# GLU weights placed elsewhere, convolution steps spread over the S5 out-projection, and the first final norm at low priority, in a hybrid convolution/S5 encoder block

## The chip, the cores and the metric

The kernel runs on one core of a Trainium2 chip. The metric is the device time of one execution in microseconds; several executions are timed and the median is given. One more execution is recorded by the hardware profiler, and all rows shown here come from that one.

## The reference

One block, batch 1, 2048 positions and 16 learned meta tokens ahead of them, model width 1024:

```
z = rms_norm(h) ;  p = z @ w_in          # columns: conv value | conv gate | S5 input, 512 each
u = v * sigmoid(gate)
y = depthwise_conv(u, width 31) + conv_b # 512 channels
conv_out = silu(layer_norm(y))           # statistics over all 512 channels of a position
s5 = gelu(S5(ssm_u) + d * ssm_u)         # bidirectional state space model
ssm_out = s5 * sigmoid(s5 @ glu_w + glu_b)
h = h + concat(conv_out, ssm_out) @ w_out
h = h + relu(rms_norm(h) @ w_ff1)^2 @ w_ff2
out = rms_norm(h)                        # meta positions dropped
```

All matrix products keep float32 accuracy: each operand is split into a high part (a cast to a shorter float, on ScalarE) and a low part (the difference, on VectorE), and three products are added (high·high, high·low, low·high).

## The kernel before

Engines are named as in the profile: PE is TensorE, DVE VectorE, ACT ScalarE, POOL GpSimd, SP the engine whose queue issues most transfers. Each engine, and each DMA queue, takes its instructions in the order in which they stand. That order is made by a scheduler: the program is written in one order, each piece gets a priority from its place there, and a piece with `tc.high_priority` is drawn forward.

The stages follow each other: input projection, S5 scan and the products for gate and value `v` (to about 495 us of the span); the stage called P3 here (495 to 820 us), which the change rewrites; then two halves of 1024 positions, each with the first FFN product (`hid_pair`), the second one (`second`) and the final norm (`final`). The first half ends at about 1505 us.

P3 works on four blocks of 512 positions (`blk` 0 to 3), and every block has four tiles of 128. Its parts are these:

- `load_glu` brings the GLU weights in by SP (`raw_gw`) and splits them into `gw` (helper `split`, lines 141 and 142).
- `conv_quad(q)`, q from 0 to 15, does the convolution of 32 channels for all positions as 12 matmuls against band matrices `cb`; four adds then write the result with its bias into the four tiles `cv`. A profile counts 24 PE records for one quad. `u8` is the input, read back from DRAM (`vdr`). `toeplitz(h)` clears a `cb` buffer and fills it with 8 transfers; one serves two quads.
- `s5_out(blk)` reads the S5 result `y`, applies the GELU (`ga`), splits it (`ghl`), multiplies by `gw` (192 matmuls `glu` over the four blocks), applies the gate (`gb`), splits again (`mhl`) and calls `wout_mm(0, ...)`.
- `wout_mm(top, blk, ...)` multiplies by one half of w_out (`woh`, `wol`, from `load_wout`; 96 matmuls `wo` for a block). Per tile it loads `xo` (the residual, 3 buffers shared with others), adds the product on DVE (line 45) and stores `xo`, to `pdr` in the S5 half (top 0) and to `hdr` in the convolution half (top 1).
- `ln_out(blk)` is the LayerNorm and swish. It needs the result of all 16 quads, since the statistics (`bn_stats`) run over all channels. It normalises `cv` (line 59), turns it by 16 transposes `tr_ln` on PE, makes `lzz` by two DVE operations (lines 59 and 45) and splits that into `zc`, the low part on POOL.
- `z_step` is the next norm with its transposes `trf` (line 836), inside the second half of w_out.

In the program before, all 16 quads are written ahead of the four `s5_out`. `gw` lies in the pool P3R, on the right side of SBUF, where the weights of the value products and their staging tiles `stv` lay. Four `cb` buffers take the tags `za` and `zb` (two each); the first half of w_out has tag `zb` too, so it waits until the quads have read `cb2` and `cb3`.

`final(half)` squares the eight accumulators `acc` on ACT, computes an inverse root on DVE, scales `acc` on DVE and stores it from SP. The FFN of the second half has its first weights (`sm`, `w`) prepared on DVE and ACT, the same engines.

Of the kernel before, what the change touches and what calls it, by code (L numbers as in the profile page):

```python
# [9 lines left out]
F32 = mybir.dt.float32  # L10
F32R = mybir.dt.float32r
# [7 lines left out]
P = 128  # L19
# [18 lines left out]
def hymba_kernel(ctx, tc, x, meta, norm_mix_g, w_in, conv_w, conv_b, conv_ln_g, conv_ln_b,  # L38
# [40 lines left out]
    def zslot(shape, name, dt=F32R, tag=None):  # L79

        if tag is None:
            tag = "zb" if nz[0] // 2 % 2 else "za"
            nz[0] += 1
        return PZ.tile(shape, dt, tag=tag, name=name, bufs=2)
# [30 lines left out]
    xv = x[0].rearrange("(c s) d -> s c d", s=NT)  # L115
# [46 lines left out]
    with ExitStack() as es2:  # L162
# [712 lines left out]
        with tc.tile_pool(name="p3", bufs=1, reuse_waits="tile") as P3:  # L875
# [3 lines left out]
            def t3(shape, name, bufs=1, dt=F32, tag=None, pool=None):  # L879
                return (pool or P3).tile(shape, dt, tag=tag or name, name=name, bufs=bufs)  # L880
# [3 lines left out]

            cv = [t3([P, 4, 512], f"cv{blk}", pool=(P3R if blk < 2 else P3)) for blk in range(4)]
            es3 = ExitStack()
            hlp = []

            def hl_tile(name):
                if not hlp:  # L890
                    hlp.append(es3.enter_context(tc.tile_pool(name="p3b", bufs=1, reuse_waits="tile")))
                return hlp[0].tile([P, 2, 512], F32R, tag="hl", name=name, bufs=9)

            def conv_quad(q):

                j = q // 4
                ps = ks_ps(f"cv{q}", [P, 4, 8, NT])
                u8 = t3([P, 4, W], f"u8_{q}", bufs=2, tag="u8", pool=P3R)
                SP.dma_start(u8, dap(vdr[j], (q % 4) * 32 * NT * W, [[W, P], [P * W, 4], [1, W]]))
                cb = toeplitz(q // 2) if q % 2 == 0 else cbs[q // 2 if q < 8 else q // 2 % 2]  # L900
                for i in range(4):
                    for m in range(3):
                        T.matmul(ps[:, i], u8[:, i, 2 - m:2 - m + P], cb[:, 4 * (q % 2) + i, :, ts(m, 16)],  # L903
                                 start=(m == 0), stop=(m == 2))
                bv = convb[:, 32 * q:32 * q + 32].rearrange("p (i c) -> p i c", c=8).unsqueeze(2)
                for blk in range(4):
                    o = cv[blk][:, :, 32 * q:32 * q + 32].rearrange("p t (i c) -> p i t c", c=8)
                    add(o, ps[:, :, :, 4 * blk:4 * blk + 4].rearrange("p i c t -> p i t c"),
                        bv.broadcast_to([P, 4, 4, 8]))
# [2 lines left out]

            def toeplitz(h):

                n = h if h < 4 else h % 2
                if h < 4:
                    cbs.append(zslot([P, 8, 8, 48], f"cb{h}", F32, tag="za" if h < 2 else "zb"))
                    (GP if h % 2 else V).memset(cbs[h], 0.0)
                for c in range(8):
                    SP.dma_start(cbs[n][16 * c:16 * c + 16, :, c, :],  # L920
                                 dap(edr[h // 2], (64 * (h % 2) + c) * 63, [[1, 16], [8 * 63, 8], [1, 48]]))
                return cbs[n]

            wo = {}

# [27 lines left out]
            def load_glu():  # L953
                for k in range(2):
                    r = raw4([P, 2, 512], f"raw_gw{k}")
                    SP.dma_start(r, glu_w[0][256 * k:256 * (k + 1), :].rearrange("(k p) n -> p k n", p=P))
                    w = t3([P, 2, 1024], f"gw{k}", dt=F32R, pool=P3R)
                    split(w[:, 0, :], w[:, 1, :], r.rearrange("p k n -> p (k n)"))
                    gw.append(w.rearrange("p a (k n) -> p a k n", k=2))

            def s5_out(blk):
                y, gh_ = [], []
                for j in range(4):
                    yy = t3([P, 512], f"y{blk}_{j}", tag="y", bufs=4)
                    SP.dma_start(yy, ydr[j][:, 4 * blk:4 * blk + 4, :].rearrange("p t c -> p (t c)"))
                    a = t3([P, 512], f"ga{blk}_{j}", tag="sg", bufs=2)
                    S.activation(a, yy, AF.Square)
                    tsc(a, a, 0.044715, ALU.mult, 1.0, ALU.add)
                    mul(a, a, yy)
                    S.activation(a, a, AF.Sigmoid, scale=1.5957691216057308)  # L970
                    mul(yy, yy, a)
                    g_ = hl_tile(f"ghl{blk}_{j}")
                    split(g_[:, 0, :], g_[:, 1, :], yy)
                    y.append(yy)
                    gh_.append(g_)
                mh = []
                for j in range(4):
                    ps = mm_ps(f"glu{blk}_{j}")
                    for k in range(4):
                        mm3(ps, gw[k // 2][:, 0, k % 2, ts(j, P)], gw[k // 2][:, 1, k % 2, ts(j, P)],  # L980
                            gh_[k][:, 0, :], gh_[k][:, 1, :], k == 0, k == 3)
                    a = t3([P, 512], f"gb{blk}_{j}", tag="sg", bufs=2)
                    S.activation(a, ps, AF.Sigmoid, bias=cols[:, 8 + j:9 + j])
                    mul(a, a, y[j])
                    m_ = hl_tile(f"mhl{blk}_{j}")
                    split(m_[:, 0, :], m_[:, 1, :], a)
                    mh.append(m_)
                wout_mm(0, blk, mh, xv, pdr)

            def ln_out(blk):  # L990
                mv = consts.tile([P, 4, 2], F32, name=f"mv{blk}", tag="mv", bufs=2)
# [22 lines left out]
                return zc  # L1014

            load_glu()
            for q in range(16):
                conv_quad(q)
                if q == 8:
                    load_wout(0)  # L1020
            load_wout(1)
            for blk in range(4):
                s5_out(blk)
            zcs = {0: ln_out(0)}
            for blk in range(4):
                if blk < 3:
                    zcs[blk + 1] = ln_out(blk + 1)
                if blk == 1:
                    esR.close()
                    PR = es5.enter_context(tc.tile_pool(name="pr", bufs=1, side="right", reuse_waits="tile"))  # L1030
                wout_mm(1, blk, zcs.pop(blk), pdr, hdr)
                if blk in (1, 2):
                    if blk == 1:
                        z_open(0)
                    for i in (0, 1) if blk == 1 else (2, 3):
                        z_step(0, i, lambda n: ks_ps(n, [P, 4, P]), lambda n: tr_ps(n, [P, 4, P]),
                               lambda q: t3([P, 512], f"zt0_{i}_{q}", tag="y", bufs=4))
# [135 lines left out]
    def final(half):  # L1173
        for t in range(8):
            n = f"{half}_{t}"
            ss, a, q, y, u, p = (consts.tile([P, 2 if i == 0 else 1], F32, tag=f"fin{i}", name=f"fin{i}_{n}", bufs=2)
                                 for i in range(6))
            h = acc[t]
            for nh in range(2):
                S.activation(junk[:, ts(nh, 512)], h[:, ts(nh, 512)], AF.Square, scale=1.0 / 32,  # L1180
                             accum_out=ss[:, nh:nh + 1])

            stt(a, ss[:, 0:1], EPS, ss[:, 1:2], ALU.add, ALU.add)
            tsc(q.bitcast(I32), a.bitcast(I32), 1, ALU.logical_shift_right)
            tsc(y.bitcast(I32), q.bitcast(I32), -1, ALU.mult, 0x5F3759DF, ALU.add)
            stt(q, y, a, y, ALU.mult, ALU.mult)
            stt(u, q, -3.0, y, ALU.add, ALU.mult)
            stt(q, u, a, u, ALU.mult, ALU.mult)
            tsc(p, q, -0.01171875, ALU.mult, 0.15625, ALU.add)
            tsc(p, p, q, ALU.mult, -0.9375, ALU.add)  # L1190
            mul(p, p, u)
            for nh in range(2):
                stt(h[:, ts(nh, 512)], h[:, ts(nh, 512)], p, gF[0][:, ts(nh, 512)], ALU.mult, ALU.mult)
                SP.dma_start(ov[8 * half + t][:, ts(nh, 512)], h[:, ts(nh, 512)])

    for half in range(2):
        with tc.tile_pool(name=f"p4_{half}", bufs=1, reuse_waits="tile") as P4:
            for p in range(NFF // 2):
                hid_pair(p, half, P4, "1267534" if p < NFF // 2 - 1 else "4312675",
                         z_late if p == 0 else None)  # L1200
        with tc.tile_pool(name=f"p5_{half}", bufs=1, reuse_waits="tile") as P5:
            second(half, P5, [(f, f + 1) for f in range(0, 8, 2)] + [(8,)] + [(f, f + 1) for f in range(9, 19, 2)] + [(19,)] +
                   [(f, f + 1) for f in range(20, 32, 2)] if half == 0 else [(f, f + 1) for f in range(0, 32, 2)])
            final(half)
    es5.close()


# [28 lines left out]
```

## Time and profile before

| what | value |
|---|---|
| three runs, us | 2186.47, 2184.84, 2182.39 (median 2184.84) |
| profiled execution, us | 2183.87, its span 2182.1 |
| PE busy | 2068.2 us (95% of the span), granted clock 0.980 on average |
| DVE busy | 1542.6 us (71%) |
| ACT, POOL busy | 710.6 us (33%), 160.5 us (7%) |

The span runs from the first to the last instruction; 1.8 us of the execution lie outside it. Busy shares are means over stages that differ: the page's slices show PE at nine tenths or more nearly everywhere, and lower ones at the beginning, around 500 to 600 us and near the final norms.

### The profile page before, as it was taken

What the parts mean: (1) busy time and instruction counts of PE and PEld (TensorE: products, weight loads), DVE (VectorE), ACT (ScalarE), POOL (GpSimd) and SP (SyncE); (2) the same over time, 40 slices, a digit from 0 to 9 for tenths busy, and PEclk for the clock granted to TensorE, in tenths of its full rate; (3) what the DMA queues carried; (4) which work ended last, traced back from release to release, by engine and by line L of the source; (5) the groups of instructions that cost most, each with busy time, mean ns of one, the idle gap of its engine ahead of it and who ended that gap; (6) DMA issues with size and microseconds to landing.
All of it is one profiled execution on the core that took longest, in us unless ns stands there. A gap on an engine that the chain in (4) does not pass through costs nothing.

```text
span 2182.1 us, 27333 instructions
## 1 busy us (share of the span) xinstructions
PE 2068.2 (95%) x10124; PEld 1694.4 (78%) x10124; DVE 1542.6 (71%) x2780; ACT 710.6 (33%) x1046; POOL 160.5 (7%) x242
## 2 busy tenths in 40 slices
PE   7989988898899999999999999997999999999997
PEld 5767777777777777888888888885888888888886
DVE  7866799963496487665558888869566656676767
ACT  5323222221143145444443222214444443111112
POOL 1031244500001110000000000000000000000000
PEclk9999999998899999999999999998999999999999
DMA  6245434423543666333345332524333235232322
GB/s 190 78 168 170 136 109 122 122 86 98 162 135 117 208 225 203 103 101 106 116 154 184 116 108 95 175 78 145 116 116 105 98 115 202 78 116 78 116 78 87
DMA packets 218509, 279.03 MB, mean 128 GB/s; under 512 B 31437, under 2 KB 164569, under 8 KB 217864
## 3 DMA queue, kind: packets, MB, share of 16 engines
q1 hardware_dynamic: 194024, 229.93, 34.2%
q10 hardware_dynamic: 23072, 43.10, 5.4%
q0 software_dynamic: 1280, 4.26, 0.5%
q8 instruction: 80, 1.31, 0.2%
q14 instruction: 53, 0.43, 0.1%
HBM read 195.39 MB, written 81.85 MB: 127 GB/s over the span
## 4 chain that ended last, share of the span: by engine, by line
PE 76%; DVE 12%; DMA 4%; issue 3%; ACT 1%; SPq 0%; ACTq 0%; POOL 0%; DVEq 0%; POOLq 0%
PE f L158 10%; PE f L159 10%; PE f L160 10%; PE ps L1093 10%; PE ps L1092 10%; PE ps L1091 9%; PE wo L158 2%; PE cv L903 2%; PE wo L160 2%; PE wo L159 2%; DMA h<-hdr 1%; DVE zo L756 1%; DVE zo L755 1%; DMA u<-udr 1%; DVE s L45 1%
## 5 line engine op out<-in xcount | busy, mean ns | idle before, releaser
L45 DVE TENSOR_TENSOR acc<-acc,f 128x512 f32<-128x512 f32 x496 | 331.7, 684 | 141.3 <-PE f L160 140.7
L158 PE MATMUL f<-w,hid 128*128 128x512 f32 x1024 | 399.9, 391 | 1.5 <-DVE acc L45 1.5
L159 PE MATMUL f<-w,hid 128*128 128x512 f32 x1024 | 398.9, 390 | 0.0
L160 PE MATMUL f<-w,hid 128*128 128x512 f32 x1024 | 398.7, 389 | 0.0
L1093 PE MATMUL ps<-zx,w 128*128 128x512 f32 x896 | 354.3, 395 | 11.7 <-DVE w L142 11.7
L1091 PE MATMUL ps<-zx,w 128*128 128x512 f32 x896 | 354.0, 395 | 5.6 <-ACT w L141 5.6
L1092 PE MATMUL ps<-zx,w 128*128 128x512 f32 x896 | 354.5, 396 | 0.0
L158 PEld LDWEIGHTS f<-w,hid 128*128 128x128 f32 x1024 | 192.3, 188 | 42.6 <-DVE acc L45 3.0
L160 PEld LDWEIGHTS f<-w,hid 128*128 128x128 f32 x1024 | 192.3, 188 | 40.1
L159 PEld LDWEIGHTS f<-w,hid 128*128 128x128 f32 x1024 | 192.3, 188 | 39.4
L1093 PEld LDWEIGHTS ps<-zx,w 128*128 128x128 f32 x896 | 169.5, 189 | 51.3 <-DVE w L142 12.7
L1091 PEld LDWEIGHTS ps<-zx,w 128*128 128x128 f32 x896 | 169.5, 189 | 45.6 <-ACT w L141 6.7
L1092 PEld LDWEIGHTS ps<-zx,w 128*128 128x128 f32 x896 | 169.4, 189 | 38.6
L141 ACT CAST hid<-rawh 128x1024 fp32r<-128x1024 f32 x64 | 67.3, 1052 | 360.9 <-PE f L160 351.5
L142 DVE TENSOR_TENSOR w<-sm,w 128x512 fp32r<-128x512 f32 x128 | 87.7, 690 | 65.9 <-ACT w L141 65.8
L141 ACT CAST w<-sm 128x512 fp32r<-128x512 f32 x128 | 78.7, 618 | 164.6 <-PE ps L1093 146.8
L141 ACT CAST w<-r 128x512 fp32r<-128x512 f32 x96 | 58.8, 616 | 130.6 <-PE ps L1093 130.5
L141 ACT CAST w<-raww 128x1024 fp32r<-128x1024 f32 x64 | 67.3, 1051 | 85.8 <-DMA raww<-in_w_ff_dram 85.8
L142 DVE TENSOR_TENSOR hid<-rawh,hid 128x1024 fp32r<-128x1024 f32 x64 | 78.2, 1222 | 15.7 <-ACT hid L141 15.7
L142 DVE TENSOR_TENSOR w<-raww,w 128x1024 fp32r<-128x1024 f32 x64 | 78.0, 1219 | 9.1 <-ACT w L141 9.1
L45 DVE TENSOR_TENSOR hh<-c,ps 128x512 f32<-128x512 f32 x64 | 44.0, 688 | 48.6 <-PE ps L1093 47.5
L45 DVE TENSOR_TENSOR xo<-xo,wo 128x512 f32<-128x512 f32 x64 | 43.8, 684 | 46.6 <-PE wo L160 43.3
(301 smaller groups left out, 3403.3 us busy)
## 6 DMA issues: line engine op xcount, KB each, us to landing
r<-in_w_ff_dram SPq DMA_DIRECT2D x64, 512.0 KB
fdr<-hh ACTq DMA_DIRECT2D x64, 512.0 KB
rawh<-fdr SPq DMA_DIRECT2D x64, 512.0 KB
raww<-in_w_ff_dram SPq DMA_DIRECT2D x64, 512.0 KB
h<-hdr SPq DMA_DIRECT2D x32, 512.0 KB
x<-in_x_dram SPq DMA_DIRECT2D x16, 512.0 KB
mt<-gdr SPq DMA_DIRECT2D x64, 128.0 KB
xo<-in_x_dram SPq DMA_DIRECT2D x16, 512.0 KB
```

The lines of the kernel that those rows point to most:

```text
L45: return V.tensor_tensor(out=o, in0=a, in1=b, op=op)
L141: S.copy(out=hi, in_=src)
L142: on.tensor_tensor(lo, src, hi.bitcast(F32), ALU.subtract)
L158: T.matmul(ps, lh, rh, start=first, stop=False)
L159: T.matmul(ps, lh, rl, start=False, stop=False)
L160: T.matmul(ps, ll, rh, start=False, stop=last)
L755: V.tensor_tensor_scan(zo[0:64, 2:4 * W + 2], f(rh)[0:64, :], f(zi)[0:64, :], 0.0, ALU.mult, ALU.add)
L756: V.tensor_tensor_scan(zo[64:128, 0:4 * W][:, ::-1], f(rh)[64:128, ::-1], f(zi)[64:128, ::-1], 0.0, ALU.mult, ALU.add)
L903: T.matmul(ps[:, i], u8[:, i, 2 - m:2 - m + P], cb[:, 4 * (q % 2) + i, :, ts(m, 16)], start=(m == 0), stop=(m == 2))
L1091: T.matmul(ps[q], w[q][:, 0, k], z[:, 0, k, :], start=(k == 0), stop=False)
L1092: T.matmul(ps[q], w[q][:, 0, k], z[:, 1, k, :], start=False, stop=False)
L1093: T.matmul(ps[q], w[q][:, 1, k], z[:, 0, k, :], start=False, stop=(k == 3))
```

## The change

The four edits are these. `gw` moves into a new pool P3G on the left side. The w_out half for the S5 part is loaded at the start and takes tag `zb`; only two `cb` buffers are left (tag `za`), and each is filled anew after the second quad that reads it. The quads are written four at a time behind the GLU of block 0 and behind the w_out products of blocks 0, 1 and 2. The final norm of the first half is wrapped in a priority with a negative offset, and its stores are issued by POOL (`GP`).

```diff
-            hlp = []
+            P3B = es3.enter_context(tc.tile_pool(name="p3b", bufs=1, reuse_waits="tile"))
+            esG = ExitStack()
+            P3G = esG.enter_context(tc.tile_pool(name="p3g", bufs=1, reuse_waits="tile"))
...
-                cb = toeplitz(q // 2) if q % 2 == 0 else cbs[q // 2 if q < 8 else q // 2 % 2]
+                cb = cbs[q // 2 % 2]
...
-                n = h if h < 4 else h % 2
-                if h < 4:
-                    cbs.append(zslot([P, 8, 8, 48], f"cb{h}", F32, tag="za" if h < 2 else "zb"))
-                    (GP if h % 2 else V).memset(cbs[h], 0.0)
+                n = h % 2
+                if h < 2:
+                    cbs.append(zslot([P, 8, 8, 48], f"cb{h}", F32, tag="za"))
+                    (GP if h else V).memset(cbs[h], 0.0)
...
+            def conv_four(n):
+                for q in range(4 * n, 4 * n + 4):
+                    conv_quad(q)
+                    if q % 2 and q < 12:
+                        toeplitz(q // 2 + 2)
...
-                    w = t3([P, 2, 1024], f"gw{k}", dt=F32R, pool=P3R)
+                    w = t3([P, 2, 1024], f"gw{k}", dt=F32R, pool=P3G)
...
-            def s5_out(blk):
+            def s5_glu(blk):
...
-                wout_mm(0, blk, mh, xv, pdr)
+                return mh
...
-            for q in range(16):
-                conv_quad(q)
-                if q == 8:
-                    load_wout(0)
-            load_wout(1)
+            load_wout(0)
+            for h in range(2):
+                toeplitz(h)
             for blk in range(4):
-                s5_out(blk)
+                mh = s5_glu(blk)
+                if blk == 0:
+                    conv_four(0)
+                if blk == 3:
+                    load_wout(1)
+                wout_mm(0, blk, mh, xv, pdr)
+                if blk < 3:
+                    conv_four(blk + 1)
...
-                SP.dma_start(ov[8 * half + t][:, ts(nh, 512)], h[:, ts(nh, 512)])
+                (SP if half else GP).dma_start(ov[8 * half + t][:, ts(nh, 512)], h[:, ts(nh, 512)])
...
-            final(half)
+            with ExitStack() if half else tc.high_priority(offset=-400):
+                final(half)
```

The scheduler decides where the instructions end up. On PE, right behind the last product `v`, the order before was this; `v3_3` is the last such product, `glu0_0` the first GLU product of block 0, and `cv0`, `cv1` are quads, of 12 matmuls each (the number behind the last underscore only tells buffers apart):

```order
L160 MATMUL v3_3_4655<-zh3_3_2182,w_v1_3_4568 128x512
L158 MATMUL glu0_0_5173<-ghl0_0_5137,gw0_4706 128x512
L159 MATMUL glu0_0_5173<-ghl0_0_5137,gw0_4706 128x512
L160 MATMUL glu0_0_5173<-ghl0_0_5137,gw0_4706 128x512
...
L158 MATMUL glu0_0_5173<-ghl0_2_5159,gw1_4711 128x512
L903 MATMUL cv0_4714<-cb0_4717,u8_0_4715 128x128 x12
L903 MATMUL cv1_4743<-cb0_4717,u8_1_4744 128x128 x12
L159 MATMUL glu0_0_5173<-ghl0_2_5159,gw1_4711 128x512
```

Of the change, PE at the first place where a quad stands, in the S5 half's w_out product of tile 0 (`wo0_0`):

```order
L159 MATMUL wo0_0_1_4986<-wol0_4721,mhl0_2_4856 128x512
L160 MATMUL wo0_0_1_4986<-woh0_4720,mhl0_2_4856 128x512
L158 MATMUL wo0_0_1_4986<-woh0_4720,mhl0_3_4875 128x512
L159 MATMUL wo0_0_1_4986<-wol0_4721,mhl0_3_4875 128x512
L903 MATMUL cv0_4878<-cb0_4738,u8_0_4879 128x128 x12
L903 MATMUL cv1_4897<-cb0_4738,u8_1_4898 128x128 x12
L160 MATMUL wo0_0_1_4986<-woh0_4720,mhl0_3_4875 128x512
```

So the GLU products of block 0 run through without a quad among them, and the quads come later, among the w_out products.

On SP, before, the first stores of `xo` (to `pdr0` and on) stood behind the loads of the last quads and of the second w_out half:

```order
L899 DMA u8_14_5063<-vdr3_84 128x4x130
L920 DMA cb1_4765<-edr3_112 16x8x48 x4
L899 DMA u8_15_5090<-vdr3_84 128x4x130
L931 DMA raw_wo1_0_5110<-in_w_out_dram 128x1024
L931 DMA raw_wo1_1_5114<-in_w_out_dram 128x1024
L931 DMA raw_wo1_2_5118<-in_w_out_dram 128x1024
L949 DMA pdr0_113<-xo0_0_5249 128x1024
L949 DMA pdr1_114<-xo0_1_5280 128x1024
L949 DMA pdr2_115<-xo0_2_5310 128x1024
L940 DMA xo0_3_5341<-in_x_dram 128x1024
```

Of the change, SP at the same stores:

```order
L936 DMA raw_wo1_1_5962<-in_w_out_dram 128x1024
L920 DMA cb0_4738<-edr1_110 16x8x48 x8
L899 DMA u8_3_4944<-vdr0_81 128x4x130
L954 DMA pdr0_113<-xo0_0_4970 128x1024
L954 DMA pdr1_114<-xo0_1_5001 128x1024
L899 DMA u8_4_5093<-vdr1_82 128x4x130
L945 DMA xo0_3_5062<-in_x_dram 128x1024
L920 DMA cb1_4748<-edr1_110 16x8x48 x8
L954 DMA pdr2_115<-xo0_2_5031 128x1024
L954 DMA pdr3_116<-xo0_3_5062 128x1024
```

The stores now stand behind the input of quad 3 only, but from here on refills of `cb` and stores alternate in the queue.

On DVE, the statistics of block 0 (`st6_0`) stood before the gate work of blocks 1 to 3, right behind the adds of quad 15 and the split of the second w_out half:

```order
L45 TENSOR_TENSOR cv3_4703<-cv15_5089,convb_4698 128x4x4x8
L142 TENSOR_TENSOR wol1_5109<-raw_wo1_0_5110,woh1_5108 128x1024
L142 TENSOR_TENSOR wol1_5109<-raw_wo1_1_5114,woh1_5108 128x1024
L142 TENSOR_TENSOR wol1_5109<-raw_wo1_2_5118,woh1_5108 128x1024
L994 BN_STATS st6_0_6098<-cv0_4700 128x6
L45 TENSOR_TENSOR xo0_3_5341<-xo0_3_5341,wo0_3_5343 128x512
L995 BN_AGGR mv0_6097<-st6_0_6098 128x2
```

Of the change, DVE at the same place:

```order
L142 TENSOR_TENSOR wol1_5957<-raw_wo1_1_5962,woh1_5956 128x1024
L45 TENSOR_TENSOR gb3_0_5893<-gb3_0_5893,y3_0_5836 128x512
L142 TENSOR_TENSOR wol1_5957<-raw_wo1_2_5966,woh1_5956 128x1024
L142 TENSOR_TENSOR mhl3_0_5896<-gb3_0_5893,mhl3_0_5896 128x512
L45 TENSOR_TENSOR gb3_1_5912<-gb3_1_5912,y3_1_5847 128x512
L999 BN_STATS st6_0_6097<-cv0_4700 128x6
L142 TENSOR_TENSOR wol1_5957<-raw_wo1_3_5970,woh1_5956 128x1024
L142 TENSOR_TENSOR mhl3_1_5915<-gb3_1_5912,mhl3_1_5915 128x512
L45 TENSOR_TENSOR gb3_2_5931<-gb3_2_5931,y3_2_5858 128x512
```

The `gb3` and `mhl3` are of block 3, and the first `xo` add behind them is that of tile 12, where it was that of tile 3. So the statistics come three blocks later against the w_out products, and those of the four blocks stand within 81 rows of DVE's order, which were 112. At the first final norm the rows of DVE, of ACT and of PE are the same in the same order before and in the change; only the 16 stores have left SP for POOL.

## Rows read from the trace of the kernel before

**Rows 1.** Windows: us, PE, PEld, DVE, ACT, POOL busy (instructions), clock, DMA, GB/s.

```profile
495.40:713.90 218.50, 195.52 (x1010) 161.90 (x1009) 134.69 (x301) 64.92 (x97) 11.64 (x8) 0.94 0.42 131
713.90:819.60 105.70, 99.58 (x466) 78.52 (x464) 73.35 (x138) 33.22 (x60) 13.11 (x11) 1.00 0.64 214
```

**Rows 2.** Timeline of PE: start, us, instruction, idle time before it and releaser.

```profile
496.81 0.50 PE L158 MATMUL glu<-ghl,gw 128*128 128x512 f32 x1 [1.19 <-ACT gw L141]
...
500.44 0.80 PE L160 MATMUL glu<-ghl,gw 128*128 128x512 f32 x1 [2.90 <-DVE gw L142]
...
505.18 7.72 PE L903 MATMUL cv<-cb,u 128*128 128x128 f32 x48 [1.07 <-DMA u<-vdr]
...
534.58 5.59 PE L903 MATMUL cv<-cb,u 128*128 128x128 f32 x48
...
579.31 5.60 PE L903 MATMUL cv<-cb,u 128*128 128x128 f32 x48 [0.41 <-DMA cb<-edr]
...
593.59 0.79 PE L158 MATMUL wo<-woh,mhl 128*128 128x512 f32 x1 [8.69 <-DVE xo L45]
...
701.62 0.66 PE L1004 MATMUL tr_ln<-ident,cv 128*128 128x128 f32 x4 [0.97 <-DVE lzz L59]
```

**Rows 3.** Timeline of ACT: the first cast of the GLU weights.

```profile
495.71 1.04 ACT L141 CAST gw<-raw_gw 128x1024 fp32r<-128x1024 f32 x1 [5.06 <-PE v L160]
```

**Rows 4.** The chain that ended last, around 580 us: start, us, what.

```profile
579.76 7.84 DMA pdr<-xo
587.61 5.15 DMA xo<-in_x_dram
```

**Rows 5.** Windows of 20 us in P3, columns as in Rows 1.

```profile
580.00:600.00 20.00, 10.12 (x56) 8.52 (x55) 12.54 (x25) 6.47 (x8) 0.00 (x0) 0.74 0.91 314
660.00:680.00 20.00, 20.00 (x88) 16.16 (x88) 8.49 (x15) 4.50 (x7) 0.00 (x0) 1.00 0.55 185
680.00:700.00 20.00, 18.69 (x94) 14.77 (x93) 17.70 (x22) 11.05 (x17) 6.94 (x5) 1.00 0.15 53
780.00:800.00 20.00, 17.10 (x84) 12.66 (x83) 18.70 (x32) 8.71 (x15) 5.51 (x4) 1.00 0.52 177
```

**Rows 6.** Longer windows of the same stage, columns as in Rows 1.

```profile
640.00:820.00 180.00, 171.41 (x789) 135.47 (x787) 124.16 (x218) 63.67 (x106) 21.56 (x16) 1.00 0.53 181
780.00:820.00 40.00, 35.76 (x171) 27.24 (x169) 36.57 (x67) 16.83 (x30) 5.51 (x4) 1.00 0.59 193
```

**Rows 7.** Groups of DVE, 600–720 and 638–820 us: busy us, mean ns, idle before.

```profile
L994 DVE BATCH_NORM_STATS2 st<-cv 128x6 f32<-128x512 f32 x12 | 8.2, 688 | 0.0
...
L45 DVE TENSOR_TENSOR lzz<-lzz,lsg 128x512 f32<-128x512 f32 x16 | 16.2, 1044 | 0.0
```

**Rows 8.** Timeline of DVE and of POOL in the LayerNorm.

```profile
686.17 0.69 DVE L45 TENSOR_TENSOR lzz<-lzz,lsg 128x512 f32<-128x512 f32 x1
...
692.72 3.11 DVE L45 TENSOR_TENSOR lzz<-lzz,lsg 128x512 f32<-128x512 f32 x2
...
692.31 2.98 POOL L142 TENSOR_TENSOR zc<-lzz,zc 128x512 fp32r<-128x512 f32 x2 [2.70 <-ACT zc L141]
```

**Rows 9.** Windows around the first final norm, columns as in Rows 1.

```profile
1484.00:1513.00 29.00, 14.07 (x47) 10.58 (x46) 28.76 (x81) 13.59 (x28) 0.00 (x0) 0.71 0.64 212
```

**Rows 10.** Timeline of PE and of DVE behind the first final norm.

```profile
1496.33 0.79 PE L1091 MATMUL ps<-zx,w 128*128 128x512 f32 x1 [5.15 <-ACT w L141]
1507.76 0.79 PE L1093 MATMUL ps<-zx,w 128*128 128x512 f32 x1 [9.78 <-DVE w L142]
...
1505.81 0.69 DVE L45 TENSOR_TENSOR sm<-r 128x512 f32<-128x512 f32 x1
```

**Rows 11.** Timeline of POOL and of ACT: a store from POOL's queue; casts behind the norm.

```profile
499.80 0.54 POOL L282 DMA_DIRECT2D vdr<-stv  x1 [1.46 <-DVE stv L45]
...
1510.50 0.61 ACT L141 CAST w<-sm 128x512 fp32r<-128x512 f32 x1
```

**Rows 12.** The chain, around 500 us: the same store from issue to landing.

```profile
499.80 2.31 DMA vdr<-stv
```

More of the change, by code (lines that the diff above doesn't have):

```diff
@@ L886, in hymba_kernel @@
             es3 = ExitStack()
-            hlp = []
+            P3B = es3.enter_context(tc.tile_pool(name="p3b", bufs=1, reuse_waits="tile"))
+            esG = ExitStack()
+            P3G = esG.enter_context(tc.tile_pool(name="p3g", bufs=1, reuse_waits="tile"))
             def hl_tile(name):
-                if not hlp:
-                    hlp.append(es3.enter_context(tc.tile_pool(name="p3b", bufs=1, reuse_waits="tile")))
-                return hlp[0].tile([P, 2, 512], F32R, tag="hl", name=name, bufs=9)
+                return P3B.tile([P, 2, 512], F32R, tag="hl", name=name, bufs=9)
             def conv_quad(q):
@@ L921, in toeplitz @@
                                  dap(edr[h // 2], (64 * (h % 2) + c) * 63, [[1, 16], [8 * 63, 8], [1, 48]]))
-                return cbs[n]
+            def conv_four(n):
[3 more added lines that the diff above has]
+                        toeplitz(q // 2 + 2)
             wo = {}
@@ L1029, in hymba_kernel @@
                     esR.close()
+                    esG.close()
                     PR = es5.enter_context(tc.tile_pool(name="pr", bufs=1, side="right", reuse_waits="tile"))
```

## The prediction

> **What bounds the kernel now.** I read the windows of the stage first, then the timeline of PE inside it, then what released PE where it waited.
>
> P3 runs from the last `v` product, about 495.4 us, to the first FFN product, 819.6 us, which is 324.2 us in all [rows 1]. PE is busy for 195.5 + 99.6 = 295.1 us of it and idle for 29.1, and the granted clock averages 0.94 in the first part and 1.00 in the second [rows 1]. So most of what can be won is idle time and slow time ahead of 714 us.
>
> How much does PE need without either? In a full window the w_out products take 20/88 = 0.227 us each [rows 5]; 768 of them give 174.6 us, and 192 GLU products at the same price 43.6. Two quads take 5.59 us [rows 2], so 16 take 44.7. Four transposes take 0.66 us [rows 2], so the 128 of `tr_ln` and `trf` take 21.1. The sum is **284.0 us**. The stage loses 324.2 − 284.0 = **40.2 us**: 29.1 idle, and 11.1 in which PE works more slowly. The same 48 quad records take 7.72 us at 505 and 5.59 us at 534 [rows 2]: 505 stands behind a row of idle times, and the window of the longest wait has a granted clock of 0.74 [rows 5]. Of TensorE's two levels, 1.2 and 2.4 GHz, such a window holds both.
>
> The largest losses have two causes. **First**, at 496.81, 500.44 and on, PE waits for `gw` [rows 2]: ACT's cast of it waits 5.06 us for the last `v` product [rows 3], because its memory only then comes free; the raw weights are not named as releaser. **Second**, at 593.59 PE waits 8.69 us for an `xo` add [rows 2]. The chain there is a store to `pdr` of 7.84 us and a load of `xo` of 5.15 us [rows 4]: the stores stand behind 16 quads' loads in SP's queue, and the fourth `xo` needs the buffer of the first. All these transfers meet in one window with a DMA share of 0.91 [rows 5].
>
> **The change part by part.**
>
> *`gw` in the S5 scan's memory.* It removes ACT's wait for the `v` product. The three idle times at 496.81, 500.44 and 505.18 are 1.19 + 2.90 + 1.07 = 5.2 us (the last is for a quad's input, and the quad is no longer there), and the quads there run 7.72 − 5.59 = 2.1 us slower. Cover: the casts need raw weights, memory and ACT, and ACT had 5 us to spare [rows 3].
>
> *Early w_out half, two `cb` buffers.* The `woh` and `wol` splits no longer wait for quad 7. They need about 4 us of ACT and DVE right behind the last `v` product; the GLU of block 0 (48 × 0.227 = 10.9 us) hides them. The price is in the refills: six, of 8 transfers each, now stand in SP's queue among the stores of `xo`. What is queued behind a refill that waits for its quad are `xo` loads and `u8` loads, and PE waits for those. The nearest row is the wait of a quad for `cb` at 579.31, 0.41 us [rows 2]. Two quads and at least part of a w_out block lie between the refill and its use, so I take nothing for four of them and 0.41 for two, 0.8; the upper bound is 1.07 (the wait for a quad's input [rows 2]) for each of six, 6.4.
>
> *Quads spread over the w_out blocks.* The `pdr` stores no longer stand behind all quad loads; this removes the 8.69 and the window's slow clock. It moves the LayerNorm: `ln_out` needs quad 15, which now stands inside the GLU of block 3. In the new order PE reaches that after 43.6 + 44.7 + 12/16 × 174.6/2 (65.5) us less the last few GLU products, about 640 us. From there the full-rate rest of the stage ends at 495.4 + 284.0 = 779.4, some 139 us later.
>
> Can DVE follow? It was busy for 124.2 us between 640 and 820 [rows 6]. What comes in from before 640: 16 `bn_stats` at 0.688 = 11.0 [rows 7], the split of the second w_out half, normalising steps and small operations of three blocks, some 14 more by my estimate from durations like these. What leaves: GLU operations of block 3 and nine `xo` adds, some 20. So about 129 us of DVE work for 139 us of PE work, 93%. The trace prices a stretch like that: from 780 to 820 DVE was 91% busy (36.57 of 40), and PE lost 4.2 of 40 us, 10.6% [rows 6]; from 680 to 700 at 89% it lost 1.3 of 20, 6.5%; from 780 to 800 at 94% it lost 2.9, 14.5% [rows 5]. I take 10.6% over 100 us (640 to about 740, where statistics, transposes and two w_out halves now meet), **10.6 us**; bounds 6.5 and 20 us (14.5% over all 139). The tail's idle time I leave as it was: 105.7 − 99.6 = **6.1 us** [rows 1].
>
> One row makes this dearer. An `lzz` product takes 0.69 us alone, but two take 3.11 us while POOL works on `zc` [rows 8], 0.87 us more each, 14 us if all 16 fell so. The Trainium skill, "SBUF — State Buffer", section "Who interferes with whom", says that a DVE instruction with two SBUF inputs contends with a GpSimd instruction that reads SBUF. The trace agrees (0.69 against 1.55). The rival "crowded LayerNorm" below works with this row.
>
> *Final norm at low priority, stores from POOL.* Behind the norm PE loses 5.15 + 9.78 us [rows 10], and in that stretch DVE is busy for 28.76 of 29 us [rows 9]; its first FFN operation comes at 1505.81 [rows 10]. A norm drawn back would free this. But the built order of DVE, ACT and PE is the same there, so I take **0**. The stores: POOL needs 0.54 us to issue one [rows 11] and it lands 2.31 us after issue [rows 12]; 16 issues are 8.6 us, spread over a norm of more than 20. Nothing else waits in POOL's queue, and SP's FFN loads get ahead, for which nobody waits here. Also 0.
>
> *Sum.* New losses 10.6 + 6.1 + 0.8 = 17.5, and 0.7 for two small waits like that of 0.41 in the GLU, where `gb` must come free: **18.2 us** instead of 40.2, a gain of **22.0**. 2183.87 − 22.0 = 2161.9. The profiled execution stands 1.0 us below the median of the runs, so I say **2162 us**.
>
> **The rivals.**
>
> *LayerNorm fits (gain 32 to 40, about 2148).* DVE's 129 us fit into 139 and PE loses only the tail's 6.1 or less. For: 660 to 680 shows DVE at 8.5 of 20 and PE full [rows 5], so much slack is there to fill. Against: DVE is in order, and an `xo` add behind a chain of statistics holds PSUM. 2183.9 − (40.2 − 6.1) = 2150, at most 2143.7 if nothing is lost.
>
> *Crowded LayerNorm (gain 4 to 13, about 2176).* The `lzz` products all meet POOL (14 us, less 16 × (1.04 − 0.69) = 5.7 that the old run already paid [rows 7], which leaves 8.3), and behind the waits the clock is at its lower level for a while, as it cost 11.1 us before. With half of those 11.1 that is 18.2 + 8.3 + 5.5 = 32.0, gain 8. For: 16 `zc` steps are pressed into less time. Against: in the second half of w_out they still have room.
>
> *Slower: refills in the queue.* If each of six refills costs what the worst queue wait of the old run did, 8.69 us [rows 2], 52 us are lost against 40.2 won, about 2196. It decides from 40.2/6 = 6.7 us each. For: refill, store and load alternate in the new order, and each waits for the one ahead. Against: only 0.41 was lost for `cb` in the old run.
>
> *Starved stores (gain about 16, 2168).* If POOL can only issue once DVE's norm ends at 1505.81, 16 × 0.54 + 2.31 put the last landing at 1516.8; the FFN weights that reuse `acc` memory are cast from 1510.50 [rows 11], some 6 us of PE. The Trainium skill has such a rule on the same page, section "SBUF: two separate sides": a DMA from GpSimd's queue gets no descriptors while DVE runs certain two-port operations, and the hardware queue is to be used. The old trace has no such store beside a busy DVE, so no run shows it yet.
>
> *The low priority takes hold (gain some 37, 2147).* It would give back 15 us at 1496 to 1508. Against it stands the unchanged order.
>
> **How the numbers follow.** No change means within 0.2%, 4.4 us, about what a measurement of this kernel can tell. Chances: the forecast 0.45 (its own range 2153 to 2170), LayerNorm fits 0.19, low priority takes hold 0.03, starved stores 0.06, crowded 0.14, within 4.4 us 0.05, slower 0.08. The range of 2146 to 2178 leaves out about 0.06 below and 0.14 above. Faster: 0.45 + 0.19 + 0.03 + 0.06 + 0.14 = 0.87; same 0.05; slower 0.08.
>
> **What would show it.** In the new profile the GLU of block 0 begins within a us of the last `v` product and runs without waits; no `xo` add is waited for longer than 2 us before 640; the clock stays at 1.0 from 495 to 640; the statistics stand at 640 to 680 with DVE over 90%; PE's waits behind 640 are for `xo`, `lzz` and `gb`; the first FFN product comes at about 797; the two waits at the final norm are there, 22 us earlier. I am wrong if quads wait for `cb` or `u8` by several us each, if DVE leaves PE idle for over 25 us behind quad 15, or if the FFN halves change by more than 2 us.

## The result, and the profile after

The changed kernel takes 2151.82 us (median of four runs, 2148.58 to 2156.70); the kernel before, run beside it, 2185.65. The ratio is 0.9849, 95% interval 0.9826 to 0.9871: 28 to 38 us faster, 33 in the middle, where 22 were forecast (2162, range 2146 to 2178). The direction and the range held; the size was too small by a third, and the time lies below the band that the forecast gave itself (2153 to 2170).

The profiled execution has a span of 2150.1 us, 32.0 less than before. The stage P3 runs from the last `v` product, which ends at 493.87, to the first FFN product at 789.48: 295.6 us where it was 324.1 (495.45 to 819.59). That is 28.5 of the 32.0. Windows of the changed kernel over the three parts of P3, with the columns of [rows 1]:

```profile
493.87:640.00 146.13, 145.75 (x832) 126.32 (x831) 79.74 (x166) 44.13 (x68) 0.54 (x1) 1.00 0.54 165
640.00:700.00 60.00, 53.79 (x241) 42.45 (x240) 56.64 (x137) 18.71 (x29) 11.40 (x8) 0.94 0.31 114
700.00:789.48 89.48, 85.11 (x404) 67.08 (x402) 68.82 (x135) 32.19 (x58) 10.60 (x8) 1.00 0.65 218
```

In the first part PE is idle for 0.4 us of 146 at full clock. Before, the clock averaged 0.94 up to 714 us and most of the 29 idle us lay there [rows 1]. What is lost now lies behind quad 15: 6.2 us idle and a clock of 0.94 between 640 and 700, then 4.4 idle us in the tail, which had 6.1 [rows 1].

The timeline of PE in the changed kernel, with the idle time before each row and its releaser: the first GLU product, then all idle times over 0.6 us up to the FFN, one shorter one of a quad, and the first FFN product.

```profile
493.64 0.39 PE L160 MATMUL v<-zh,w_v 128*128 128x512 f32 x1
493.87 0.39 PE L158 MATMUL glu<-ghl,gw 128*128 128x512 f32 x1
...
632.01 2.92 PE L903 MATMUL cv<-cb,u 128*128 128x128 f32 x24 [0.38 <-DVE cv L45]
...
670.05 0.50 PE L158 MATMUL wo<-woh,zc 128*128 128x512 f32 x1 [0.79 <-ACT zc L141]
...
677.51 0.41 PE L1009 MATMUL tr_ln<-ident,cv 128*128 128x128 f32 x2 [2.86 <-DVE cv L59]
...
689.50 0.50 PE L158 MATMUL wo<-woh,zc 128*128 128x512 f32 x1 [0.64 <-DVE xo L45]
...
692.84 0.66 PE L1009 MATMUL tr_ln<-ident,cv 128*128 128x128 f32 x2 [1.92 <-DVE cv L59]
...
742.20 0.50 PE L158 MATMUL wo<-woh,zc 128*128 128x512 f32 x1 [1.26 <-DVE xo L45]
...
762.92 0.50 PE L160 MATMUL wo<-woh,zc 128*128 128x512 f32 x1 [0.72 <-POOL zc L142]
...
785.98 0.50 PE L158 MATMUL wo<-woh,zc 128*128 128x512 f32 x1 [0.78 <-DVE xo L45]
...
789.48 0.50 PE L1102 MATMUL ps<-zx,w 128*128 128x512 f32 x1 [0.48 <-ACT w L141]
```

The GLU follows the `v` product without a gap, where PE waited 1.19, 2.90 and 1.07 us [rows 2]. No row waits for `cb`, `u8` or `gw`, and the 8.69 us for an `xo` add [rows 2] are gone. Two shorter waits of the kernel before, which the prediction does not price, are gone as well, another one for `gw` and one for the low part of the w_out half that is now early:

```profile
503.31 0.80 PE L158 MATMUL glu<-ghl,gw 128*128 128x512 f32 x1 [0.79 <-ACT gw L141]
...
542.28 0.50 PE L159 MATMUL wo<-wol,mhl 128*128 128x512 f32 x1 [2.11 <-DVE wol L142]
```

The longest that are left in P3 are two waits for the normalising step of the LayerNorm (line 59). At the first final norm nothing has changed; the same two waits as in [rows 10] are there, earlier:

```profile
1465.44 0.79 PE L1102 MATMUL ps<-zx,w 128*128 128x512 f32 x1 [5.14 <-ACT w L141]
1476.86 0.79 PE L1104 MATMUL ps<-zx,w 128*128 128x512 f32 x1 [9.77 <-DVE w L142]
```

The remaining 3.5 us of the 32.0 lie before P3 (1.6) and behind it (1.9), in stages whose instructions on PE and DVE stand in the same order. Over the twelve profiles of this study the last `v` product ended between 491.45 and 496.18, and over the eight in which nothing is moved behind P3 but the norm's priority and stores, the time from the first FFN product to the end was 1360.0 to 1363.0 (the kernel before: 1362.5, the changed one: 1360.6). I count these 3.5 us as scatter.

### The profile page after: what moved, and what is told of

It is laid out like the page before. It is cut to its first block, busy times and chain, and to the rows that moved or that the text cites. A ratio compares the mean times of both kernels' runs of the same rounds, so it can differ in the third digit from the quotient of the medians.

```text
span 2150.1 us, 27315 instructions
## 1 busy us (share of the span) xinstructions
PE 2050.0 (95%) x10124; PEld 1682.7 (78%) x10124; DVE 1542.8 (72%) x2779; ACT 709.8 (33%) x1046; POOL 168.9 (8%) x257
## 4 chain that ended last, share of the span: by engine, by line
PE 78%; DVE 12%; DMA 3%; issue 2%; ACT 1%; ACTq 0%; SPq 0%; DVEq 0%
PE f L158 10%; PE f L159 10%; PE f L160 10%; PE ps L1104 10%; PE ps L1103 10%; PE ps L1102 10%; PE wo L158 2%; PE wo L160 2%; PE wo L159 2%; PE cv L903 2%; DMA h<-hdr 1%; DVE zo L756 1%; DVE s L45 1%; DVE zo L755 1%; DVE r L45 1%
```

## The experiments

Where a ratio is given, it is that to the kernel before, run on the same chip, with its 95% interval.

**GLU weights alone.** The kernel before with `gw` in the new pool (the lines that open and close the pools are left out):

```diff
...
-                    w = t3([P, 2, 1024], f"gw{k}", dt=F32R, pool=P3R)
+                    w = t3([P, 2, 1024], f"gw{k}", dt=F32R, pool=P3G)
```

> The kernel before with one part of the change alone: the GLU weights in the new left pool. Theory, the parts add up: the three idle times at 496 to 505 us (5.2 us) and the slow quads there (2.1 us) go, the 8.7 us wait for the xo add at 593 stays as it is; about 7 us faster than before, 2178. Rival, the parts overlap: what is saved at 500 is waited for again at the xo add, whose transfers do not come earlier; that wait grows to 12 to 15 us and the gain is under 2 us.

2176.16 us, ratio 0.9970 (0.9958 to 0.9982): 6.6 us faster, by the interval 3.9 to 9.2. PE at the start of the GLU, and at the old `xo` wait:

```profile
496.49 0.50 PE L158 MATMUL glu<-ghl,gw 128*128 128x512 f32 x1 [0.84 <-ACT gb L983]
...
584.02 0.79 PE L158 MATMUL wo<-woh,mhl 128*128 128x512 f32 x1 [8.54 <-DVE xo L45]
```

No wait for `gw` is left, and the wait for `xo` is as long as it was (8.54, before 8.69). From the last `v` product to that row it is 91.3 us here and 98.1 before, so 6.9 us are won, as the theory has it. The whole of P3 is only 4.1 us shorter in this profile (320.1 against 324.1), since 2.8 us are lost again behind that row.

**GLU weights put back.** The changed kernel with `gw` in the old pool again; the other new pool stays.

> The changed kernel with the GLU weights back in the old right-side pool, all else as changed. Theory, the parts add up: PE waits for gw again behind the last v product, some 5 to 7 us slower than the changed kernel (2158), no wait for xo before 640. Rival: without quads among the first GLU products nothing fills the time until the second gw half can be split (its memory waits for the store of the last v tile), and the loss is 10 us or more (2162 and up).

2160.28 us, ratio 0.9884 (0.9863 to 0.9905); 7.9 us slower than the kernel of the next experiment, which has the new place and ran on the same chip. The four runs lie far apart (2154.40 to 2165.84), and the profile is that of the longest. PE and the windows of 20 us at the start:

```profile
497.20 0.50 PE L158 MATMUL glu<-ghl,gw 128*128 128x512 f32 x1 [1.84 <-ACT gw L141]
...
498.65 0.79 PE L160 MATMUL glu<-ghl,gw 128*128 128x512 f32 x1 [0.71 <-DVE gw L142]
```

```profile
480.00:500.00 20.00, 17.44 (x71) 13.42 (x70) 7.95 (x8) 4.05 (x6) 3.75 (x3) 0.95 0.20 55
500.00:520.00 20.00, 19.96 (x102) 16.24 (x101) 13.75 (x22) 11.37 (x18) 0.00 (x0) 0.88 0.74 211
```

Two waits of 2.6 us in all, then a granted clock of 0.88: TensorE is at its lower level for a part of that window. So this part of the change is worth 6.6 us alone and about 8 in company, which the scatter does not tell apart, and the rest of the change, without it, 25 us (2183.59 − 0.9884 × 2183.59 = 25.3).

**Final norm put back.** The changed kernel with the stores on SP and no priority:

```diff
-                (SP if half else GP).dma_start(ov[8 * half + t][:, ts(nh, 512)], h[:, ts(nh, 512)])
+                SP.dma_start(ov[8 * half + t][:, ts(nh, 512)], h[:, ts(nh, 512)])
...
-            with ExitStack() if half else tc.high_priority(offset=-400):
-                final(half)
+            final(half)
```

> The changed kernel with the final norm of the first half as before: normal priority, stores from SP. Theory: the priority moves nothing on DVE, ACT and PE, and no store is waited for, so the time is that of the changed kernel within 0.2% (2152 plus or minus 4), with waits of 5.1 and 9.8 us behind the norm in both. Rival: the stores on POOL's queue let the FFN loads of the second half go ahead and give 1 to 3 us, which come back here.

2152.35 us, ratio 0.9856 (0.9841 to 0.9870): the time of the changed kernel. Neither the priority nor the queue of these stores is worth anything here.

**Stores from ACT's queue.** The kernel before with one edit in `wout_mm`:

```diff
-                    SP.dma_start(dst[t], xx)
+                    (SP if top else S).dma_start(dst[t], xx)
```

> The kernel before with one edit: the stores of xo to pdr are issued from ACT's queue instead of SP's; quads, GLU weights and buffers as before. Theory, the queue: the 8.7 us wait at 593 comes from stores that stand behind quad and weight loads on SP; it shrinks to under 2 us and the slow clock behind it goes; about 10 us faster than before, 2175. Rival, the transfers: the window is full of transfers (share 0.91), the xo load is late whichever queue stores; the wait stays above 6 us and the gain is under 3 us.

2184.74 us, ratio 1.0008 (0.9999 to 1.0018): no gain, so the rival's time, but by neither mechanism. PE:

```profile
586.78 0.79 PE L158 MATMUL wo<-woh,mhl 128*128 128x512 f32 x1 [2.92 <-DVE xo L45]
...
597.52 0.80 PE L158 MATMUL glu<-ghl,gw 128*128 128x512 f32 x1 [6.18 <-ACT ghl L141]
```

The wait for `xo` does shrink, to 2.92 us, and what it gave back is waited for 11 us later at the start of block 1, for `ghl` (6.18). PE had no other work left: all quads were done. So the queue made most of the wait for `xo`, and without it PE is held up one step later. The edit has a side effect: ACT, which casts `ghl`, now holds the stores in its own queue and issues one at 592.10; what that adds to the new wait is not separated.

**Low part of `zc` on DVE.** The changed kernel with POOL taken out of the LayerNorm:

```diff
-                        split(z_[:, 0, :], z_[:, 1, :], zz, GP)
+                        split(z_[:, 0, :], z_[:, 1, :], zz)
```

> The changed kernel with one edit: the low part of zc in the LayerNorm is computed on DVE, POOL computes nothing there. Theory, the neighbour: DVE operations with two inputs stretch while POOL works on zc (lzz products 1.2 to 1.8 us instead of 0.69, small ones 1.25 instead of 0.15 us); without POOL they are short again, and PE's waits of 2.9 us at 677 and 1.9 us at 693 shrink below 1 us, in spite of 16 more operations of 0.6 us; time 2146 to 2151. Rival, DVE is simply full between 640 and 700 us: 10 us more work make it later, time 2155 to 2162.

2147.34 us, ratio 0.9838 (0.9823 to 0.9852), by the medians about 4.5 us faster than the changed kernel, whose interval this one overlaps (0.9826 to 0.9871). P3 bears the gain out: it is 288.6 us long here and 288.8 in the last run below, which has the same edit, against 293.9 to 296.6 in the five other runs that have the changed kernel's P3. First the changed kernel's timeline of DVE and POOL where PE waits 2.86 us:

```profile
670.08 6.01 POOL L142 TENSOR_TENSOR zc<-lzz,zc 128x512 fp32r<-128x512 f32 x4 [174.19 <-ACT zc L141]
...
671.34 2.38 DVE L45 TENSOR_TENSOR lzz<-lzz,lsg 128x512 f32<-128x512 f32 x2
673.65 1.25 DVE L45 TENSOR_TENSOR rst_ln<-rsy_ln,rst_ln 128x4 f32<-128x4 f32 x1
674.82 0.16 DVE L58 TENSOR_SCALAR rst_ln<-rsa_ln 128x4 int32<-128x4 int32 x1
674.93 1.18 DVE L62 SCALAR_TENSOR_TENSOR rsy_ln<-rst_ln,rsu_ln 128x4 f32<-128x4 f32 x1
```

An operation on 128 x 4 elements takes 1.25 us, the one behind it, with one input, 0.16. That is not a rule for one input: beside POOL's next operations another one-input row takes as long.

```profile
689.57 2.84 POOL L142 TENSOR_TENSOR zc<-lzz,zc 128x512 fp32r<-128x512 f32 x2 [1.28 <-ACT zc L141]
...
689.97 1.25 DVE L58 TENSOR_SCALAR rsy_ln<-rsy_ln 128x4 f32<-128x4 f32 x1
```

The group of `lzz` products, first in the changed kernel, then without POOL, and the window of 640 to 700 us without POOL:

```profile
L45 DVE TENSOR_TENSOR lzz<-lzz,lsg 128x512 f32<-128x512 f32 x16 | 13.0, 845 | 0.0
...
L45 DVE TENSOR_TENSOR lzz<-lzz,lsg 128x512 f32<-128x512 f32 x16 | 10.4, 687 | 0.0
```

```profile
640.00:700.00 60.00, 59.10 (x279) 46.76 (x278) 58.97 (x151) 21.01 (x33) 0.00 (x0) 1.00 0.40 140
```

Without POOL all 16 products are short. DVE is busier (58.97 of 60 us against 56.64), and PE is idle for 0.9 us instead of 6.2, at full clock. So a full DVE alone does not make PE wait. But that DVE comes earlier without its neighbour is not what the rows show. The two normalising steps that PE waits for, and PE's transposes behind them, first in the changed kernel, then without POOL:

```profile
676.82 1.91 DVE L59 TENSOR_SCALAR cv<-cv,mv,rsy_ln 128x512 f32<-128x512 f32 x4
691.25 2.81 DVE L59 TENSOR_SCALAR cv<-cv,mv,rsy_ln 128x512 f32<-128x512 f32 x4
```

```profile
676.26 1.00 DVE L59 TENSOR_SCALAR cv<-cv,mv,rsy_ln 128x512 f32<-128x512 f32 x2
691.27 1.00 DVE L59 TENSOR_SCALAR cv<-cv,mv,rsy_ln 128x512 f32<-128x512 f32 x2
...
677.00 0.38 PE L1009 MATMUL tr_ln<-ident,cv 128*128 128x128 f32 x2
691.99 0.38 PE L1009 MATMUL tr_ln<-ident,cv 128*128 128x128 f32 x2
```

The first step begins only 0.6 us earlier, the second not earlier at all: what DVE no longer loses beside POOL it spends on the subtractions. What changed is PE's order, which the scheduler built anew. From 669 us on, 16 w_out products with `zc` stand ahead of the first of these transposes, where 7 stood, and 72 ahead of the second, where 46 stood. At 0.227 us each (the price in the prediction) these are 2.0 and 5.9 us of work that PE has while DVE gets there; up to the two transposes PE is idle for 2.7 and 5.3 us less than in the changed kernel. By these rows the gain lies mainly in the order; a run with the one order and the other engine was not made. Behind 700 us the idle time grows (6.8 us against 4.4); P3 as a whole is 7.0 us shorter by these profiles, of which the medians show 4.5.

**Quads earlier.** The changed kernel with all quads behind the GLU and the w_out products of blocks 0 and 1:

```diff
-                if blk == 0:
-                    conv_four(0)
+                if blk < 2:
+                    conv_four(2 * blk)
...
-                if blk < 3:
-                    conv_four(blk + 1)
+                if blk < 2:
+                    conv_four(2 * blk + 1)
```

> The changed kernel with the quads in groups of four behind the GLU and behind the w_out products of blocks 0 and 1, so that the last one comes near 600 instead of 640 us. Theory, the LayerNorm is crowded behind the last quad: its statistics now spread over blocks 2 and 3, the idle 6 us between 660 and 700 and the slow clock there go; 2143 to 2147. Rival, the quads are the filler that covers the steps from block to block: without them PE waits for ghl and xo at the starts of blocks 2 and 3 and the refills come closer together; 2150 to 2158.

2154.39 us, ratio 0.9869 (0.9854 to 0.9884): no gain, the rival's band. PE at the step to block 2 and in the w_out products of block 3:

```profile
603.95 0.50 PE L158 MATMUL glu<-ghl,gw 128*128 128x512 f32 x1 [2.23 <-ACT ghl L141]
...
667.69 0.50 PE L158 MATMUL wo<-woh,mhl 128*128 128x512 f32 x1 [1.98 <-DVE xo L45]
```

Two waits are back, at steps where the changed kernel has none: one for `ghl`, with three quads still to come (from 613.12 on), and one for `xo`, when no quad is left. The theory holds in part: between 640 and 700 PE's idle time falls from 6.2 to 4.2 us and the clock stays at 1.00 there. Together nothing is won.

**First FFN pair ahead of the norm.** To see what a norm that really comes late would bring: the changed kernel with the weights and six of the seven products of the second half's first pair written ahead of `final(0)`, in tiles of the pool that is still open (`hid`, `w2`, free by then; the lines of `hid_pair` that do this are left out):

```diff
...
+            if half == 0:
+                pre = hid_pair(0, 1, None, "1267534", z_late, P5=P5)
             with ExitStack() if half else tc.high_priority(offset=-400):
                 final(half)
```

> The changed kernel in which the weights and six of seven products of the first FFN pair of the second half stand ahead of the first final norm, in memory of the stage before that is free by then, so that the norm really comes late. Theory: PE's waits of 5.1 and 9.8 us behind the norm and the slow clock there go; 14 to 18 us faster than the changed kernel, 2134 to 2138. Rival, DVE is the limit there (28.8 of 29 us busy): the norm and the next pair's weights only change places, PE waits for the second pair instead, and the gain is under 5 us.

2152.43 us, ratio 0.9868 (0.9851 to 0.9884): no gain. The two waits behind the norm are gone; another stands in their place, 8 us behind the second of them. PE, the cast that it waits for, DVE there, and the chain:

```profile
1485.13 0.80 PE L1065 MATMUL ps<-zx,w 128*128 128x512 f32 x1 [8.71 <-ACT w L141]
...
1484.46 1.14 ACT L141 CAST w<-r 128x512 fp32r<-128x512 f32 x2 [13.43 <-DMA out_dram<-acc]
...
1484.51 0.69 DVE L45 TENSOR_TENSOR sm<-r 128x512 f32<-128x512 f32 x1 [6.56 <-DMA out_dram<-acc]
```

```profile
1478.24 6.05 DMA out_dram<-acc
```

DVE was idle for 6.56 us there, so it was not the limit: the second pair's weights had got memory in which `acc` had lain, and waited for the norm's last store, 6.05 us from issue to landing.

**The same with other memory.** Added to the edit of the run before: two tiles are claimed first, so that the second pair's weights lie where `hid` and `w2` were:

```diff
...
+            hold = P4.tile([P, 4, 4, P], F32, tag="sm", name=f"sm_{n}", bufs=1)
+            S.copy(out=hold[:, 0, 0, 0:1], in_=r2[:, 0, 0:1])
+            hold = P4.tile([P, 2, 4, P], F32R, tag="w", name=f"w_{n}", bufs=6)
+            S.copy(out=hold[:, 0, 0, 0:1], in_=r2[:, 0, 0:1])
```

> As the run with the first pair ahead of the norm, but with the second pair's weights in memory that the last products free, not in that of acc (there they waited for the norm's last store, which landed 6 us after its issue). Theory, it was the memory: PE's wait of 8.7 us shrinks below 3 us, and the version is 9 to 13 us faster than the changed kernel, 2139 to 2143. Rival, DVE is the limit: PE waits just as long for weights that DVE makes behind the norm, and the time stays at 2150 or above.

2138.23 us, ratio 0.9783 (0.9764 to 0.9802), 13 to 14 us faster than the changed kernel. One wait of 2.23 us is left. PE's row, the window around it, and last the changed kernel's window at the same place:

```profile
1475.05 0.50 PE L1067 MATMUL ps<-zx,w 128*128 128x512 f32 x1 [2.23 <-DVE w L142]
```

```profile
1455.00:1485.00 30.00, 27.64 (x118) 21.68 (x117) 27.53 (x74) 12.83 (x23) 6.50 (x12) 1.00 0.71 228
```

```profile
1455.00:1485.00 30.00, 15.08 (x55) 11.40 (x54) 29.53 (x81) 12.92 (x26) 6.47 (x12) 0.72 0.70 219
```

In the same 30 us PE is busy for 12.6 us more, and the clock stays at its upper level (1.00 against 0.72).

**The same with the stores on SP.** One edit, `SP.dma_start` for the norm's stores.

> The same with the norm's stores issued from SP's queue. Theory, a store from POOL's queue is late beside a busy DVE: the stores land earlier from SP and what waits for acc memory comes 2 us or more earlier than in the version with POOL. Rival, the queue does not matter for landing, and on SP the stores stand ahead of the FFN loads of the second half: same time or 1 to 4 us slower.

2138.82 us, ratio 0.9785 (0.9770 to 0.9800): the same. The queue of these stores does not matter here, where PE no longer waits for one of them.

**Both.** That version, stores from POOL, with the low part of `zc` on DVE:

> The version with the first pair ahead of the norm and its memory mended, and the low part of zc on DVE instead of POOL. Theory: the two gains lie in different stages and add up, 13 to 17 us faster than the changed kernel, 2135 to 2139. Rival: what is saved is lost to scatter or to a wait between the stages, and the time is that of the better of the two alone.

2133.01 us, ratio 0.9762 (0.9746 to 0.9779): 5 us below the version without the second edit, 19 below the changed kernel and 52 below the kernel before. The gains add up (13.6 and 4.5 us by the medians). It is the fastest version of this study.

## Why the prediction came out as it did

- **What bounds the kernel** was read rightly: most of what P3 lost lay ahead of 714 us, as idle and slow time, and up to 640 us the changed kernel loses 0.4 us.
- **The number and the bands.** At 2151.82 us the time lies outside the forecast's own band (2153 to 2170) and in that of the rival "LayerNorm fits" (a gain of 32 to 40). That rival has the number, not the mechanism: PE did lose 10.3 us between 640 and 700, and the rest of the difference is in the terms below and in scatter.
- **The sum of 284.0 us at full rate** was too large by about 3.5 us. In the changed kernel PE is busy for 145.75 + 53.79 + 85.11 = 284.65 us, and the version without POOL, with the same work and a clock of 1.00 in all three such windows, for 145.68 + 59.10 + 75.72 = 280.5. So the work takes about 280.5, and by this difference 4.1 us of the changed kernel's were slow clock. I had priced 16 quads at 5.59 us for two, from a row behind which PE waits (2.11 us, at 542.28); in the changed kernel the next product follows two quads after 5.27 us (510.26 to 515.53), 2.6 us less for all. The rest of the 3.5 must lie in the other prices and is not traced.
- **`gw`: 5.2 + 2.1 us.** Right as far as the runs can tell: 6.6 alone, 7.9 the other way round. A fourth idle time there, of 0.79 us at 503.31, was left out.
- **Early w_out half and two `cb` buffers: 0.8 us.** Nothing waited. The rival of refills in the queue, which was to end slower, found no support: not one row waits for `cb` or `u8`. What this part gives was not priced apart: the wait of 2.11 us for `wol` at 542.28 is gone.
- **Quads spread over the w_out blocks.** The new losses were put at 18.2 us (two waits of 0.41 make 0.8, not 0.7) and came to 15.1: 11.0 idle (60 − 53.79, 89.48 − 85.11 and 0.4) and 4.1 of slow clock. The crowd between 640 and 740 was priced at 10.6 and cost 10.3, which is luck: the price was idle time alone, of which there were 6.2 us, and the 4.1 of slow clock were no term of it. The tail was left at 6.1 and cost 4.4; the small waits, put at 1.5, cost 0.4. With the 3.5 of the sum these are 6.6 of the 10 us by which the forecast fell short; the other 3.5 lie in stages that are the same.
- **Why that wait goes away** was told too simply. I had said that the stores no longer stand behind the quads' loads. The run with the stores on ACT shows that taking them out of that queue gives nothing by itself: the wait turns into one for `ghl`. In the changed kernel quads, which wait for nothing of the block's chain, stand at every step from block to block, and no such wait is left. The run with earlier quads agrees: at two steps waits of 2.23 and 1.98 us are back, though most of the gain stays. No run spreads the quads and leaves the stores behind the loads, so how the 25 us are shared between the queue and the quads is not shown.
- **The crowd's cause.** I priced it by DVE's busy share. The run without POOL shows that this share does not set the loss: with DVE at 98% of 640 to 700 PE lost 0.9 us. The rival's row, a product held up beside POOL (0.69 against 1.55 [rows 8]), is there, but costs little: the 16 `lzz` products took 13.0 us in the changed kernel, against 10.4 without POOL and 16.2 before [rows 7]. By the Trainium skill, "SBUF — State Buffer", section "Who interferes with whom", an operation with two SBUF inputs and a GpSimd instruction that reads SBUF contend; the row of 1.25 us at 673.65 agrees. What most decides here is how many products stand in PE's order between one normalising step and the next.
- **The signs.** The GLU, the waits ahead of 640, the clock there and DVE's share came as foretold, the two waits at the norm are there, and the FFN halves changed by 1.9 us. The first FFN product came at 789.48 and not at about 797, the norm's waits stand 31 us earlier and not 22, and the longest waits behind 640 are for line 59, which the list did not name.
- **Starved stores.** The same page of the Trainium skill, section "SBUF: two separate sides", warns of a store from GpSimd's queue while DVE runs a two-port operation. In this kernel the queue made no difference, neither as it was (2152.35 against 2151.82) nor with the first pair ahead of the norm and its memory mended (2138.82 against 2138.23). In the one run in which PE waits for the norm's last store, SP's queue was not tried, and no row tells whether DVE runs such an operation in this norm.
- **Low priority: 0.** Right: the kernel with the norm put back takes the same time. With the pair's weights in tiles of the open pool, the order changes and the two waits go; the priority alone moved no row. The weights' pool is opened behind `final`, and the scheduler placed nothing of it ahead. That this is the rule by which it decides is read from the program and these orders, not tested apart. The 15 us that I had put on such a norm were a fair price (13 to 14 measured), but only once the next weights no longer lay in `acc`'s memory.

## What to carry to other kernels

Work that waits for nothing (here the convolution) can cover the steps at which another chain goes from block to block; try to spread it there instead of running it ahead, and ask of each wait what PE could do meanwhile as well as what makes it. Here a priority moved nothing while the memory of the work that should pass was given out later: place the memory first, then look at the built order. And an edit on one engine can change the order on another: the subtractions put back on DVE, 10 us of them, cost nothing in this place, and the gain beside them came mainly with a new order on PE. Compare the orders before a gain is put down to the engine that was edited.

## What was not expected of the hardware

A DVE operation on four elements per partition took 1.25 us instead of 0.15 while POOL computed, once with two inputs and once with one. Its own size does not explain that; POOL's operations there take 1.3 to 1.5 us each, so that it waited for one of them to end would fit, but no row shows it. And the norm's stores of 256 KB took 2.5 us from issue to landing in the changed kernel (median of 16, the longest 5.9), but 4.6 in the run with the first pair ahead of the norm (the longest 6.7, the last 6.05). FFN loads run beside the stores in both; what makes the difference was not tested.
